# Six pairs of the attention's output columns by seven products, with sums and forms on POOL, and two merge columns moved

## The chip, the cores and the metric

The kernel runs on one core of a Trainium2 chip. The metric is device time in microseconds for one execution. The engines are named as in the profile: PE is TensorE (matmuls), DVE is VectorE, ACT is ScalarE, POOL is GpSimd, SP is SyncE, which here issues the DMA transfers. SBUF is the on-chip memory that the engines work in, PSUM the banks in which PE adds up products.

## The reference

One layer of a hybrid encoder in fp32, for 512 prompt tokens and 8 x 16 sample tokens; the kernel takes them as T = 640 columns. Cut to what matters:

```
z = x @ w_in                                   # x: 640 x 2048
y_a = (fox_attention(q, k, v, f) * silu(gate_a)) @ w_out_fox     # 1024 -> 2048
y_b = (gated_delta(conv(qkv), g, beta) * silu(gate_b)) @ w_out_gdn   # 1024 -> 2048
h = (sigmoid(m_a) * y_a + sigmoid(m_b) * y_b) @ w_out            # 2048 -> 2048
x1 = layer_norm(alpha * x + h)
out = x1 + sigmoid(x1 @ w_pl_gate) * rms_norm(p @ w_pl_proj)
```

Both branches have 8 heads of 128. The delta branch solves a triangular system per chunk and head and carries a state from chunk to chunk. m_a and m_b, the merge gates, are columns of the first product.

## The kernel before, in words

**Products.** Activations lie with features on the 128 partitions and the 640 tokens along the free dimension, in two halves of 320. Every fp32 operand is split in a rounded part (a cast on ACT) and the rest (a subtraction on DVE): `split`, L333 and L334, makes xh and xl of a tile of activations; `w_piece`, L305 and L306, makes wh and wl of a weight piece of 128x512. A product of two tiles is three matmuls: wh by xh, wh by xl, wl by xh.

**Weights** come as halves of 512 KB (`wr`, three buffers, L252, issued by SP), in an order fixed by `plan`. `w_ahead`, called ahead of each k-tile, starts a load when a buffer is free and cuts pieces up to five (`PIECES`) ahead of their use.

**Columns.** `column` (L359 and L360) makes one block of 128 output features: 16 k-tiles by 3 matmuls by 2 token halves, 96 matmuls. `pair` (L433) makes two blocks by Strassen's and Winograd's seven products in place of eight: the operands are four sub-blocks of activations and sums of them (X11, X21, X22 and T1 to T4, called forms), and four sums of weight halves (S1, S2, b, S3). The results are added up on DVE (L442). In the kernel before, the front, w_out and the gate use `pair`; weight sums of the front are made on DVE, those of the later pairs ahead of time on POOL (`weight_sums`, L272), by way of DRAM.

**Stages.** The front; the attention with its 8 heads; the delta branch (`phase_gdn`), for each of 8 heads four columns and one merge column (`mcol`, `FILL` = 1); two more merge columns; the attention's output columns (w_out_fox, K = 1024), 16 blocks, each 48 matmuls in a group of 8 k-tiles, copied by ACT (`kept`, tile fx, L1522) and stored in DRAM (fd); then the delta output columns, w_out, norm and gate.

**Order.** Beside PE's columns run generators: conv_silu, the head's preparation (`gdn`), its blocks (`gdn_blocks`), its chunks (`gdn_chunks`), the output norm. `tick`, once per k-tile or so, steps them when a clock kept while the program is built (`saw` adds a cost for each instruction, `watch` compares) says that what they issue will be ready. On the chip there are only in-order queues and semaphores. `gdn_blocks` is the one the change and the prediction touch: it writes the lower blocks to DRAM and reads them back as `lanes`, runs a scan of 31 steps on DVE (two operations each, L933 and L935, sx and sx2, ever shorter), writes the result (`xd<-sx`, L941), reads it back as u0 (L944) and loads the state (L948). Behind it in `gdn_chunks` each chunk makes right sides rp (L1110) and the state S (L1124) on DVE, for which PE's small matmuls wait.

The inputs of the output columns, the heads' results og, are kept in DRAM (`ogd`); 16 tiles are reloaded (`ogr<-ogd`, L1492) and split.

Of the kernel before, what the change touches and what calls it, by code (L numbers as in the profile page):

```python
# [52 lines left out]
class Kernel:  # L53
# [9 lines left out]
    PAIR0, PAIRS = 10, 4 + FRONT // 2  # L63
    FILL = 1
    GATES = 6
    FREE = 0.5
    LATE = 3
# [9 lines left out]
    def saw(self, ins):  # L77
# [14 lines left out]
        if e == 3:  # L92
# [101 lines left out]
    def plan(self):  # L194
# [4 lines left out]
        self.ops, self.halves, c = [], [], 0  # L199
        self.wsums, self.later = {}, [*range(n - 32, n - 16, 2), *range(n - 16 + self.GATES, n, 2)]  # L200
        while c < n:
            if c in self.later:
# [31 lines left out]
            c += len(cs)  # L234
        self.raw, self.wq, self.used = {}, {}, 0
        self.rest = 0
        self.nh = self.no = self.np = 0

    def w_new(self, tag):
        pool = self.wp if tag == "wr" else self.zp  # L240
        return pool.tile([P, 1024], F32, tag=tag, name=tag, bufs=3)

    def w_tile(self):
        c, hf, tag, uses = self.halves[self.nh]
        self.nh += 1
        self.raw[c, hf] = [self.w_new(tag), uses, tag]
        return c, hf

# [31 lines left out]
    def w_free(self, tag):  # L280
        return sum(v[1] > 0 for v in self.raw.values() if v[2] == tag) < 3

# [26 lines left out]
    def w_ahead(self):  # L309

        if self.nh < len(self.halves) and self.now >= self.rest and self.w_free(self.halves[self.nh][2]):
            self.w_load()
        if self.no == len(self.ops):
            return
        o = self.ops[self.no]
        if o[0] == "s":
            if o[2] in self.raw and o[3] in self.raw and (o[1] in self.raw or self.w_free("sr")):
                self.no += 1
                self.w_sum(*o[1:])
        elif self.np - self.used < self.PIECES and o[1] in self.raw:  # L320
            self.w_piece()
# [5 lines left out]

    def split(self, src):

# [3 lines left out]
        nc.scalar.copy(out=hi, in_=src)  # L333
        nc.vector.tensor_tensor(out=lo, in0=src, in1=hi.bitcast(F32), op=ALU.subtract)  # L334
        return hi, lo
# [75 lines left out]

    def pair(self, xf, fin, each=None, uv=None):


        nc = self.nc
        c = self.col
        self.col += 2
        u, v = uv or (self.zt([P, HALF], "u"), self.zt([P, HALF], "v"))
        banks = {}

        def run(i, form, bank, more=False):
            if not more:
                banks[bank] = self.gps(xf[form][0][0].shape[-1])
            ps = banks[bank]
            for k in range(8):
                if each:
                    each(i, k)
                self.w_ahead()
                wh, wl = self.wq[(c, i), k // 4]
                w = slice((k % 4) * P, (k % 4) * P + P)  # L430
                xh, xl = xf[form][k]
                for n, (a, b) in enumerate(((wh, xh), (wh, xl), (wl, xh))):
                    nc.tensor.matmul(ps, a[:, w], b, start=(k == 0 and n == 0 and not more), stop=(k == 7 and n == 2),  # L433
                                     skip_group_check=True)
# [9 lines left out]
        w = body(u)  # L444
        add(w, w, run(1, "T2", "b"))
        fin(0, 0, run(2, "X21", "a", True))
        add(v, w, body(run(3, "T3", "d")))
# [469 lines left out]
    def gdn_blocks(self, h, kq, lt, qk, qg, kt, vr, cs):  # L917
# [30 lines left out]
        nc.sync.dma_start(out=st, in_=self.i["st"][h])  # L948
        yield 8
        self.chunks["gens"].append(self.gdn_chunks(h, kq, lt, qk, qg, kt, vr, cs, u0, st))  # L950

# [16 lines left out]
    def gdn_out(self, h, ob, cs):  # L968
# [30 lines left out]
        if h < 7:  # L999
            nc.sync.dma_start(out=self.ogd[8 + h], in_=og)  # L1000
        else:
            self.op[15] = self.split(og)
        self.gdone = h
# [436 lines left out]
    def phase_gdn(self, conv, work):  # L1440
# [6 lines left out]
        self.sums["gens"].append(self.weight_sums([ws[:, x:x + 171] for x in range(0, 684, 171)], slice(8, None),  # L1447
                                                  (10, 8, 5)))
        self.uu = self.zt([P, 5, P], "uu")
# [9 lines left out]
        self.gdone = -1  # L1459
        self.scaled, self.chdone = False, -1  # L1460
        self.ends["gens"].append(self.scale_e(re))
        self.untapped = 0
        for h in range(H):
# [24 lines left out]
        due = deque()  # L1488

        def load(k, tag):  # L1490
            raw[k] = self.zt([P, T], tag, 1, "ogr")
            nc.sync.dma_start(out=raw[k], in_=self.ogd[k])  # L1492
            if k < 8:
                due.append((self.now + 8, k))

        def each1(s):
# [3 lines left out]
            if s in (8, 10, 12):  # L1500
                load((s - 8) // 2, tags[(s - 8) // 2])
        tags = "strip", "cy", "sg"

        def take():
            k = due.popleft()[1]
            nop[k] = self.split(raw[k])
            if k + 3 < 8:
                load(k + 3, tags[k % 3])

        def after(s):  # L1510
            if due and due[0][0] <= self.now and due[0][1] <= s:
                take()
        self.mcol("cth", each=each1)
        self.mcol("cth", after=after)
# [4 lines left out]
        def kept(ps):  # L1519
# [4 lines left out]
            self.nf += 1  # L1524
        for n in range(8):
            def each(s):
                while n == 0 and due and (due[0][0] <= self.now or due[0][1] <= s):
                    take()
                k = 8 + n
                if s == 1 and n < 7:  # L1530
                    self.until(lambda: self.gdone >= n)
                    load(k, ("sg", "cth")[n % 2])
                if s == 13 and n < 7:
                    nop[k] = self.split(raw[k])
# [587 lines left out]
def _layout(a):  # L2122
# [13 lines left out]
          for g in range(2)]  # L2136
    nf, r = Kernel.FRONT, Kernel.FILL
    bl += [bq[0], bk[0], *bv[0], *bv[1]]
# [9 lines left out]
    for h in range(H):  # L2148
        bl += [gq[h], gv[h], gk[h], gg[h]]
        if h < 7:  # L2150
            bl += m[nf + 3 + r * h:nf + 3 + r * (h + 1)]
    bl += m[nf + 3 + 7 * r:]
    for n in ("w_out_fox", "w_out_gdn"):
        wo = _wblock(a[n][0])
        bl += [np.concatenate([wo[2 * i], wo[2 * i + 1]], 1) for i in range(8)]
    for b in _wblock(a["w_out"][0]):
# [71 lines left out]
```

## Time and profile before

| what | us |
|---|---|
| runs shown, median (lowest to highest) | 2203.46 (2202.28 to 2206.6) |
| profiled execution, its own time | 2205.76 |
| span of the profile | 2202.9 |
| PE busy in the span | 2186.2 |
| DVE / ACT / POOL busy | 1488.9 / 901.3 / 317.0 |

| stretch of the span, us | DVE busy | ACT busy | POOL busy |
|---|---|---|---|
| 950 to 1540, delta heads and merge columns | 426.89 | 254.78 | 97.17 |
| 1540 to 1667, attention's output columns | 64.96 | 47.48 | 12.83 |
| 1667 to 2203, the rest | 436.25 | 230.75 | 64.54 |

The profile is of one execution; the granted TensorE clock was 0.998 over it. A row of a group says line, engine, operation, out<-in, shapes and count, then busy time and mean ns of one, then the engine's idle time just before and what ended it. In a timeline the first number is the start, the second the length, and x2 means that two neighbours are shown as one.

### The profile page before, as it was taken

To read this page: it belongs to the slowest core of one execution; us is meant where nothing else is said; L and a number is where in the kernel's file an instruction comes from. 1 tells how busy PE (TensorE), PEld (TensorE's weight loads), DVE (VectorE), ACT (ScalarE), POOL (GpSimd) and SP (SyncE) were. 2 spreads that over 40 slices of the span, in tenths; PEclk is the share of its full clock that TensorE was granted. 3 is DMA by queue.
4 is the path that set the end of the run, shared out by engine and by line. 5 is a ranking of instruction groups with operands and counts; after the bars stand their busy time and mean duration, and the time that the engine had idled before them with its cause. 6 is when DMAs were issued, how large, how long until landed. Compare 5 with 4: busy or idle time off the path is not lost. (4 is left out here: it accounts for less than half of the span.)

```text
span 2202.9 us, 41346 instructions
## 1 busy us (share of the span) xinstructions
PE 2186.2 (99%) x15586; PEld 2110.7 (96%) x15586; DVE 1488.9 (68%) x3055; ACT 901.3 (41%) x2007; POOL 317.0 (14%) x530
## 2 busy tenths in 40 slices
PE   9999999999999999999999999999999999999998
PEld 7889999999999999999999999999999999999998
DVE  5377777664454446666776866767645787789997
ACT  4244444443333335334434534435332243354544
POOL 0003222220101000111111211111100000021222
PEclk9999999999999999999999999999999999999999
DMA  6336555657877657834434434446646656673465
GB/s 234 125 123 196 190 187 190 198 187 247 274 232 264 226 173 242 282 107 139 139 114 137 132 107 142 126 123 193 196 151 216 220 160 210 193 274 130 147 227 170
DMA packets 205799, 403.25 MB, mean 183 GB/s; under 512 B 32392, under 2 KB 104152, under 8 KB 205600
## 3 DMA queue, kind: packets, MB, share of 16 engines
q1 hardware_dynamic: 205600, 400.62, 56.4%
q8 instruction: 122, 2.00, 0.4%
q14 instruction: 77, 0.63, 0.1%
HBM read 310.97 MB, written 89.56 MB: 182 GB/s over the span
## 5 line engine op out<-in xcount | busy, mean ns | idle before, releaser
L306 DVE TENSOR_TENSOR wl<-wr,wh 128x512 fp32r<-128x512 f32 x634 | 457.3, 731 | 367.8 <-ACT wh L305 362.2
L305 ACT CAST wh<-wr 128x512 fp32r<-128x512 f32 x634 | 389.1, 620 | 379.5 <-PE g L360 156.1
L359 PE MATMUL g<-xh,wh 128*128 128x320 f32 (+1 forms) x1312 | 427.2, 326 | 0.8 <-ACT xh L333 0.4
L359 PE MATMUL g<-xl,wh 128*128 128x320 f32 (+1 forms) x1312 | 405.9, 309 | 0.5 <-DVE xl L334 0.5
L360 PE MATMUL g<-xh,wh 128*128 128x320 f32 x1312 | 405.8, 309 | 0.0
L360 PE MATMUL g<-xl,wh 128*128 128x320 f32 x1312 | 405.5, 309 | 0.0
L359 PE MATMUL g<-xh,wl 128*128 128x320 f32 (+1 forms) x1312 | 405.4, 309 | 0.0
L360 PE MATMUL g<-xh,wl 128*128 128x320 f32 x1312 | 405.2, 309 | 0.0
L433 PE MATMUL g<-xh,wh 128*128 128x320 f32 (+1 forms) x864 | 267.6, 310 | 2.6 <-ACT u L443 1.1
L433 PE MATMUL g<-xl,wh 128*128 128x320 f32 (+1 forms) x864 | 267.7, 310 | 0.6 <-DVE xl L334 0.6
L433 PE MATMUL g<-xh,wl 128*128 128x320 f32 (+1 forms) x864 | 267.5, 310 | 0.0
L359 PEld LDWEIGHTS g<-xh,wh 128*128 128x128 f32 x1312 | 247.3, 189 | 13.8 <-issue 9.5
L360 PEld LDWEIGHTS g<-xh,wh 128*128 128x128 f32 x1312 | 247.5, 189 | 0.9
L359 PEld LDWEIGHTS g<-xl,wh 128*128 128x128 f32 x1312 | 247.2, 188 | 1.1 <-DVE xl L334 1.1
L360 PEld LDWEIGHTS g<-xl,wh 128*128 128x128 f32 x1312 | 247.0, 188 | 0.0
L359 PEld LDWEIGHTS g<-xh,wl 128*128 128x128 f32 x1312 | 246.6, 188 | 0.2 <-DVE wl L306 0.2
L360 PEld LDWEIGHTS g<-xh,wl 128*128 128x128 f32 x1312 | 246.7, 188 | 0.0
L272 POOL TENSOR_TENSOR ws<-ws 128x171 f32<-128x171 f32 (+2 forms) x176 | 128.0, 727 | 809.3 <-DMA ws<-in_w 800.8
L433 PE MATMUL g<-t,wh 128*128 128x320 f32 (+1 forms) x848 | 187.7, 310 | 0.4 <-ACT t L2045 0.4
L433 PEld LDWEIGHTS g<-xh,wh 128*128 128x128 f32 x864 | 162.6, 188 | 3.5 <-ACT u L443 1.4
L433 PEld LDWEIGHTS g<-xl,wh 128*128 128x128 f32 x864 | 162.4, 188 | 1.2 <-DVE xl L334 1.1
L433 PEld LDWEIGHTS g<-xh,wl 128*128 128x128 f32 x864 | 162.7, 188 | 0.0
(425 smaller groups left out, 3469.8 us busy)
## 6 DMA issues: line engine op xcount, KB each, us to landing
wr<-in_w SPq DMA_DIRECT2D x263, 512.0 KB, 3.8
kc<-in_kc SPq DMA_DIRECT2D x32, 512.0 KB, 7.4
vc<-in_vc SPq DMA_DIRECT2D x32, 512.0 KB, 5.8
ws<-in_w SPq DMA_DIRECT2D x80, 128.0 KB, 2.5
md<-m SPq DMA_DIRECT2D x32, 320.0 KB, 2.3
t<-md SPq DMA_DIRECT2D x32, 320.0 KB, 4.6
ws<-in_w SPq DMA_DIRECT2D x100, 85.5 KB, 3.4
t<-rr SPq DMA_DIRECT2D x24, 320.0 KB, 5.5
```

The source lines that it names most:

```text
L272: nc.gpsimd.tensor_tensor(out=o, in0=x, in1=y, op=op)
L305: nc.scalar.copy(out=hi, in_=src)
L306: nc.vector.tensor_tensor(out=lo, in0=src, in1=hi.bitcast(F32), op=ALU.subtract)
L359: nc.tensor.matmul(ps[0], whl[w], xhl[o][:, a], start=(first and x == 0), stop=(last and x == 2))
L360: nc.tensor.matmul(ps[1], whl[w], xhl[o][:, b], start=(first and x == 0), stop=(last and x == 2))
L433: nc.tensor.matmul(ps, a[:, w], b, start=(k == 0 and n == 0 and not more), stop=(k == 7 and n == 2), skip_group_check=True)
```

## The change

1. `FILL` becomes a table for each head: heads 5 and 6 lose their merge column, which then run behind head 7's columns, ahead of the two that were there.
2. The first two of the eight pairs of attention's output blocks stay plain (`PLAIN`). The other six run as half pairs: `pair(half=True)`, seven products of 4 k-tiles, 84 matmuls for two blocks. The order of products is X11, T2, T1, T3, X21, X22, T4.
3. The four weight sums of each half pair are made on POOL, 128x512 each (`m_sum`), just ahead of use, into tiles that earlier work has left (`ws`, `sg` and the raw halves, later loads of which go to `kq0` and `lanes`).
4. The forms are made by a new generator, `forms`: it reloads eight og tiles, makes four sums of 128x320 for each two k-tiles on POOL (`form_sums`), and splits them on ACT, DVE and POOL (`form_splits`).
5. Of the delta branch's og tiles, reloaded during the half pairs, those of even index are split in the last half pair with the rest on POOL; the last head's og is split after the loop. The clock's cost of a POOL operation and the waits of `weight_sums` change, and with them where generators are stepped.

```diff
-    FILL = 1
+    FILL = 1, 1, 1, 1, 1, 0, 0, 4
+    PLAIN = 2
...
-        a, b = ((0.17, 0.0011), (0.21, 0.00085), (0.25, 0.0020))[e]
+        a, b = ((0.17, 0.0011), (0.21, 0.00085), (0.13, 0.0032))[e]
...
+            if n - 48 + self.PLAIN <= c < n - 40:
+                j = c - (n - 48 + self.PLAIN)
+                self.halves += [(c, 0, "wr", 5), (c, 1, "wr" if j < 2 else ("kq0", "lanes")[j % 2], 3)]
+                for key, p, i in (((c, 0), 0, 0), ((c, "S2"), 0, 1), ((c, "S1"), 0, 4), ((c, "b"), 0, 3),
+                                  ((c, 0), 1, 2), ((c, "S3"), 0, 6), ((c, 1), 1, 5)):
+                    self.ops.append(("p", key, p, ((c, i), 0)))
+                self.sumq += [(c, x) for x in ("S1", "S2", "b", "S3")]
...
+    def m_sum(self):
+        c, name = self.sumq[0]
...
+        lo, hi = slice(0, 512), slice(512, 1024)
+        a = self.w_use((c, 0)) if name != "S1" else None
+        b = self.w_use((c, 1)) if name in ("S1", "b") else None
...
+        self.raw[c, name] = [out, uses, "m"]
+        self.nc.gpsimd.tensor_tensor(out=out, in0=x, in1=y, op=op)
+        self.made[c, name] = self.busy[2] + 0.3
...
+        if half:
+            add(v, w, run(4, "T1", "c"))
+            add(v, v, run(3, "T3", "d"))
+            fin(1, 1, v)
+            fin(0, 0, run(2, "X21", "a", True))
+            fin(0, 1, run(6, "X22", "c", True), u)
+            fin(1, 0, run(5, "T4", "d", True), u)
+            return
...
-            for _ in range(self.FILL if h < 7 else 0):
+            for _ in range(self.FILL[h] if h < 7 else self.FILL[7] - 2):
                 self.mcol("sg")
...
+        def form_sums(k):
+            a, b = fr[2 * k], fr[2 * k + 1]
+            for o, x, y, op in ((b[:, xb], b[:, xb], a[:, xb], ALU.subtract), (a[:, xb], a[:, xb], a[:, xa], ALU.subtract),
+                                (a[:, xa], b[:, xb], a[:, xa], ALU.add), (b[:, xa], b[:, xa], a[:, xa], ALU.subtract)):
+                nc.gpsimd.tensor_tensor(out=o, in0=x, in1=y, op=op)
+        def form_splits(k):
+            a, b = fr.pop(2 * k), fr.pop(2 * k + 1)
+            th, tl = self.split(b, nc.gpsimd)
...
+            for t, sl in ((t1, xb), (t2, xa)):
+                nc.scalar.copy(out=t[:, xa], in_=a[:, sl])
+                nc.vector.tensor_tensor(out=t[:, xb], in0=a[:, sl], in1=t[:, xa].bitcast(F32), op=ALU.subtract)
...
-        for n in range(8):
+        for n in range(self.PLAIN):
...
+        self.until(lambda: len(xf["X11"]) == 4)
...
+        for n in range(self.PLAIN, 8):
...
+            self.pair(xf, kept2, each, uv=(uv, fx[1][:, xb]), half=True)
+            self.nf += 2
```

The change moves instructions on three engines in one place, the last delta head's scan. In what follows, lines of the kernel before and of the change differ in number: L933 and L935 are now L992 and L994, L941, L944 and L948 now L1000, L1003 and L1007, L252 is L267, L306 is L351, L272 is L287.

POOL, around head 7's scan, before (uu and kpad are copies for a head's chunks, vm is a masked product, ws a weight sum):

```order
L962 COPY uu<-u_17721 32x5x32 x4
L272 TENSOR_TENSOR ws<-ws 128x171 x2
L1026 TENSOR_TENSOR vm<-vnd,cb 128x256
L272 TENSOR_TENSOR ws<-ws 128x171 x10
L957 COPY kpad<-kq_9603 128x4x16 x2
```

The same place now:

```order
L1022 COPY uu<-u_17819 32x5x32 x4
L1592 TENSOR_TENSOR ogr<-ogr 128x320 x4
L1086 TENSOR_TENSOR vm<-vnd,cb 128x256
L1592 TENSOR_TENSOR ogr<-ogr 128x320 x4
L381 TENSOR_TENSOR xl<-ogr,xh 128x640 x2
L339 TENSOR_TENSOR s_18308<-wr 128x512
L339 TENSOR_TENSOR s_18320<-s_18308,wr 128x512
L339 TENSOR_TENSOR wr<-wr 128x512
L1592 TENSOR_TENSOR ogr<-ogr 128x320 x4
L339 TENSOR_TENSOR s_18320<-wr,s_18320 128x512
L1592 TENSOR_TENSOR ogr<-ogr 128x320 x4
L381 TENSOR_TENSOR xl<-ogr,xh 128x640 x2
```

The form sums (L1592), their splits (L381) and the first half pair's weight sums (L339) stand where twelve sums of 128x171 stood; those now stand ahead.

DVE, the part of head 7's scan in which the chunks of head 6 are made, before:

```order
L1124 SCALAR_TENSOR_TENSOR S<-S,gl,s 128x128
L306 TENSOR_TENSOR wl<-wr,wh 128x512
L933 TENSOR_TENSOR sx_18263<-sx,lanes 80x8x27
L935 TENSOR_TENSOR sx<-sx,sx_18263 80x8x27
L933 TENSOR_TENSOR sx_18263<-sx,lanes 80x8x26
L935 TENSOR_TENSOR sx<-sx,sx_18263 80x8x26
L1110 SCALAR_TENSOR_TENSOR rp<-s,negc,vr 128x128
```

The same now:

```order
L1182 COPY S<-s 128x128
L1107 SCALAR_TENSOR_TENSOR st<-st,glb,s 128x128 x4
L1602 TENSOR_TENSOR t_18232<-ogr,t_18232 128x320
L1602 TENSOR_TENSOR t_18233<-ogr,t_18233 128x320
L992 TENSOR_TENSOR sx_18146<-sx,lanes 80x8x25
L994 TENSOR_TENSOR sx<-sx,sx_18146 80x8x25
L992 TENSOR_TENSOR sx_18146<-sx,lanes 80x8x24
L994 TENSOR_TENSOR sx<-sx,sx_18146 80x8x24
L351 TENSOR_TENSOR wl<-wr,wh 128x512
L1170 SCALAR_TENSOR_TENSOR rp<-s,negc,vr 128x128
```

The splits of t1 and t2 (L1602) and the state updates st now stand between the scan's steps and ahead of rp.

SP, from the scan's write to the weight loads, before:

```order
L941 DMA xd<-sx 80x256
L252 DMA wr<-in_w 128x1024
L1523 DMA fd_18012<-fx 128x640
L944 DMA u_18679<-xd 128x5x32
L948 DMA st<-in_st 128x1024
```

The same now:

```order
L1000 DMA xd<-sx 80x256
L1193 DMA out_stp<-S 128x128
L1032 DMA og<-sgd_174 128x640
L1003 DMA u_18682<-xd 128x5x32
L1007 DMA st<-in_st 128x1024
L267 DMA wr<-in_w 128x1024 x2
```

A weight half that stood between write and read-back is now behind both and the state's load.

More of the change, by code (lines that the diff above doesn't have):

```diff
@@ L424, in run @@
             ps = banks[bank]
-            for k in range(8):
+            last = 3 if half else 7
+            for k in range(last + 1):
                 if each:
@@ L432, in run @@
                 for n, (a, b) in enumerate(((wh, xh), (wh, xl), (wl, xh))):
-                    nc.tensor.matmul(ps, a[:, w], b, start=(k == 0 and n == 0 and not more), stop=(k == 7 and n == 2),
+                    nc.tensor.matmul(ps, a[:, w], b, start=(k == 0 and n == 0 and not more), stop=(k == last and n == 2),
                                      skip_group_check=True)
@@ L1001, in gdn_out @@
         else:
-            self.op[15] = self.split(og)
+            self.last = og
         self.gdone = h
@@ new lines, in forms @@
+        def forms():
+            while self.sums["gens"]:
+                yield 1
+            load2(0, "ws")
+            load2(1, "og")
+            while self.done[0] < 7:
+                yield 1
+            load2(2, "dt")
+            load2(3, "v")
+            yield 4
+            form_sums(0)
+            yield 2
+            form_sums(1)
+            yield 2
+            while self.op is not nop or due:
+                yield 1
+            load2(4, "cth")
+            form_splits(0)
+            load2(5, "og")
+            self.formed = True
+            yield 1
+            form_splits(1)
+            load2(6, "dt")
+            load2(7, "v")
+            yield 5
+            form_sums(2)
+            yield 1
+            form_sums(3)
+            form_splits(2)
+            yield 1
+            form_splits(3)
+            yield 1
@@ L1524, in kept @@
             self.nf += 1
-        for n in range(8):
+        for n in range(self.PLAIN):
             def each(s):
-                while n == 0 and due and (due[0][0] <= self.now or due[0][1] <= s):
+                while n == 0 and due and (due[0][0] <= self.now or order[due[0][1]] <= s):
                     take()
[L1529 to L1534, printed above, removed]
-            self.column(groups=((0, 8), (8, 16)), base=0, each=each, done=kept)
+            self.column(groups=((0, 8), (8, 16)), base=0, each=each, done=kept)
@@ new lines, in store, with each @@
+        def store():
+            while late:
+                i, t = late.popleft()
+                nc.sync.dma_start(out=self.fd[i], in_=t)
+        again = dict(zip(range(8, 15), ("dt", "v", "kt", "vr", "lt", "qk", "gr")))
+        for n in range(self.PLAIN, 8):
+            def each(i, k):
+                if (i, k) == (1, 0):
+                    store()
+                if n in (5, 6) and k == 0 and i in (2, 3, 4, 5):
+                    x = 4 * n - 14 + i
+                    if x < 15:
+                        self.until(lambda: self.gdone >= x - 8)
+                        load(x, again[x])
+                if n == 7 and k == 2 and i in (1, 4, 3, 2):
+                    x = {1: 8, 4: 10, 3: 12, 2: 14}[i]
+                    nop[x] = self.split(raw[x], nc.gpsimd)
+                if n == 7 and i == 5:
+                    x = 9 + 2 * k
+                    if x < 15:
+                        nop[x] = self.split(raw[x])
+            fx[1] = self.zt([P, T], "cy", 1, "fx")
+            self.pair(xf, kept2, each, uv=(uv, fx[1][:, xb]), half=True)
+            self.nf += 2
@@ L1536, in phase_gdn @@
+        store()
+        self.until(lambda: self.gdone == 7)
+        nop[15] = self.split(self.last)
         self.until(lambda: self.gdone == 7 and not self.sums["gens"])
```

113 lines of the change are left out of this document (88 added, 25 removed).

## The prediction

> **What bounds the kernel now.** I read the page's busy shares first, then the chain of waits, then the windows over the stage that is changed, and last the timelines of the two engines that share work there.
>
> ```profile
> span 2202.9 us, 41346 instructions
> PE 2186.2 (99%) x15586; PEld 2110.7 (96%) x15586; DVE 1488.9 (68%) x3055; ACT 901.3 (41%) x2007; POOL 317.0 (14%) x530
> ```
>
> TensorE (PE) is busy for 2186.2 of 2202.9 us. Fewer matmuls are therefore worth their whole time, and every new wait of PE is lost whole. The price of one matmul stands in the chain of waits (start, us, what), where PE runs products of the pair form without a break:
>
> ```profile
> 1809.22 170.03 PE g L433 x1158
> ```
>
> That is 170.03 / 1158 = 0.147 us for a matmul of 320 columns. The stage that changes is the attention's output columns and the end of the last delta head, from about 1500 to 1670 us. Its windows show (range, length, then busy us and count of PE, PEld, DVE, ACT, POOL, then clock, DMA share, GB/s):
>
> ```profile
> 1500.00:1550.00 50.00, 49.83 (x398) 46.68 (x397) 33.15 (x100) 28.26 (x77) 9.19 (x17) 1.00 0.69 210
> 1550.00:1600.00 50.00, 50.00 (x397) 49.47 (x395) 36.80 (x108) 19.70 (x53) 7.45 (x16) 1.00 0.64 197
> 1600.00:1650.00 50.00, 50.00 (x371) 47.99 (x364) 18.85 (x50) 19.74 (x54) 2.98 (x5) 1.00 0.47 153
> ```
>
> PE is full, at a granted clock of 1.00. VectorE (DVE) has 17 and 13 us of 50 free up to the end of the last head's scan, and 31 after it; GpSimd (POOL) does almost nothing.
>
> **The matmuls.** Each of the six half pairs runs seven products of 4 k-tiles by 3 matmuls, 84, where two plain columns ran 96. The small matmuls stay in number, and so do the merge columns, which only change place. So 6 x 12 = 72 matmuls go: 72 x 0.147 = **-10.6 us**. Heads 5 and 6 lose 96 matmuls (14.1 us) of PE work each, under which DVE works. By the row of 1500 to 1550 DVE is busy for two thirds of the time there, so I cost the loss of this cover at nothing; if it is short, PE waits in those heads for states or pieces, up to 2 us.
>
> **Steady work of the half pairs.** DVE cuts seven pieces a pair instead of four, ScalarE (ACT) too:
>
> ```profile
> L306 DVE TENSOR_TENSOR wl<-wr,wh 128x512 fp32r<-128x512 f32 x74 | 51.9, 701 | 61.8 <-ACT wh L305 60.9 <-DMA wr<-in_w 0.7
> L764 DVE SCALAR_TENSOR_TENSOR sg<-sc,sg 128x320 f32<-128x320 f32 x2 | 1.0, 491 | 0.1
> L272 POOL TENSOR_TENSOR ws<-ws 128x171 f32<-128x171 f32 x100 | 67.1, 671 | 224.7 <-DMA ws<-in_w 219.2
> L2042 POOL TENSOR_TENSOR t<-t 128x640 f32<-128x640 f32 x20 | 36.2, 1815 | 68.5 <-DMA t<-rr 37.1 <-DVE wl L306 15.4 <-DVE t L2010 15.1
> ```
>
> A pair lasts 84 x 0.147 = 12.3 us on PE. DVE needs 7 x 0.70 for pieces and at most 7 x 0.49 for additions of 320 columns, 8.3 us; ACT is given three casts more, and had 30 of 50 us free in the row of 1600. POOL makes four sums of 128x512. No such POOL row exists: between 0.671 us (171 columns) and 1.815 us (640) a straight line gives 1.50, so 6.0 us a pair. The last pair has four lo splits of 640 columns on POOL instead, 7.3 us. All of it fits under 12.3 us of PE, so I cost it at nothing; if the first splits of the next column come late there, PE loses 1 to 2 us. The eight reloads of 320 KB lie ahead of their readers by ticks of the plan and cost nothing either, unless SP is held up (below).
>
> **The stretch in which the forms are made** is another matter. Between the start of head 7's scan and the last form split (t2 of the fourth k pair, which the first half pair's second product, T2, needs), the order has 174 matmuls of 320 columns and 25 small ones on PE; on DVE 56 scan operations, 7 pieces, 8 splits of 320 and 15 operations of 128x128; on POOL 8 form sums of 320, 4 weight sums of 512 and 4 splits of 640. The rows for these:
>
> ```profile
> 1062.34 0.38 PE L1106 MATMUL s<-S,kq 128*128 128x128 f32 x2
> L933 DVE TENSOR_TENSOR sx<-eye,lanes 80x248 f32<-80x248 f32 x1 | 0.4, 405 | 0.0
> L933 DVE TENSOR_TENSOR sx<-sx,lanes 80x32 f32<-80x32 f32 x1 | 0.2, 188 | 0.0
> L1110 DVE SCALAR_TENSOR_TENSOR rp<-s,negc,vr 128x128 f32<-128x128 f32 x3 | 1.0, 344 | 1.7 <-PE s L1106 1.7
> ```
>
> PE: 174 x 0.147 + 25 x 0.19 = 30.3 us. DVE: the scan shortens from 0.405 to 0.188 us an operation, 56 x 0.297 = 16.6, and 7 x 0.70 + 8 x 0.49 + 15 x 0.344 = 14.0, together 30.6 us. So DVE has no spare time here, where it had a quarter in the rows above. And the two engines hold each other up. Both timelines (start, us, engine, line, xcount) are of the kernel before:
>
> ```profile
> 1060.88 2.02 POOL L272 TENSOR_TENSOR ws<-ws 128x171 f32<-128x171 f32 x3
> ...
> 1061.27 0.60 DVE L933 TENSOR_TENSOR sx<-sx,lanes 80x152 f32<-80x152 f32 x1
> ...
> 1062.54 0.53 DVE L933 TENSOR_TENSOR sx<-sx,lanes 80x144 f32<-80x144 f32 x1
> ...
> 1063.10 0.30 DVE L935 TENSOR_TENSOR sx<-sx,sx 80x144 f32<-80x144 f32 x1
> ```
>
> ```profile
> 2085.79 3.79 POOL L2042 TENSOR_TENSOR t<-t 128x640 f32<-128x640 f32 x2 [0.18 <-DMA t<-rr]
> 2086.08 4.05 DVE L306 TENSOR_TENSOR wl<-wr,wh 128x512 fp32r<-128x512 f32 x2
> ...
> 2089.93 3.60 POOL L2042 TENSOR_TENSOR t<-t 128x640 f32<-128x640 f32 x2 [0.35 <-DMA t<-rr]
> 2090.45 3.63 DVE L306 TENSOR_TENSOR wl<-wr,wh 128x512 fp32r<-128x512 f32 x2
> 2090.67 0.39 PE L433 MATMUL g<-xh,wh 128*128 128x320 f32 x1 [0.94 <-ACT t L2045]
> ```
>
> A scan operation takes 0.60 beside a POOL sum of 171 columns and 0.30 without: 0.3 us lost for each. A piece takes 2.03 beside a POOL operation of 640 columns instead of 0.70: 1.33 lost. On the line between them 320 columns cost 0.63 and 512 cost 1.05. The 16 POOL operations then cost 8 x 0.63 + 4 x 1.05 + 4 x 1.33 = 14.6 us, if DVE always stands at an operation with two inputs in SBUF. The scan, the pieces and the splits are that, 25.4 of 30.6 us, the 128x128 ones read PSUM; so 14.6 x 0.83 = 12.1. DVE ends 12.4 us behind PE's 30.3. How much of that PE bears: in the second timeline DVE lost (4.05 + 3.63) - 4 x 0.70 = 4.9 us, and PE's own gap, 0.94, was for another engine. I let PE bear 4.9 and take **+7.5 us**, with 0 and 12.4 as its bounds. What comes late is the states and right sides of head 6's chunks (S, rp), for which PE stands, and behind them in DVE's queue its pieces and t2. A single rule of the Trainium skill speaks to this more strictly; it stands with the rivals.
>
> **The weight load behind the scan's end.** In the new order the load of the second half pair's half stands on SP behind the scan's write, the og load, the read-back and the state load; before, it stood ahead of the read-back. SP's waits, from the chain:
>
> ```profile
> 1514.41 3.44 DMA xd<-sx
> ...
> 1517.87 0.37 SPq L944
> ...
> 1518.28 1.16 SPq L948
> ...
> 1519.54 5.50 DMA wr<-in_w
> ```
>
> That landing is a long one by the page's list of transfers (last column: median us to landing):
>
> ```profile
> wr<-in_w SPq DMA_DIRECT2D x263, 512.0 KB, 3.8
> ```
>
> From the scan's end to the landed half: 3.44 + 0.37 + 1.16 + 3.8 to 5.5, 8.8 to 10.5 us. Then S1 and S2 on POOL (3.0) and the cast on ACT (0.6, estimated from DVE's 0.70) make 12.4 to 14.1. The scan ends six scan operations and a piece after t2 is split, 6 x 0.19 + 0.70 = 1.8 us. From T2 of the first pair, where it needs that t2, to T2 of the second PE has 74 matmuls, 10.9 us. So PE waits 1.8 + 12.4 - 10.9 = 3.3 to 5.0 us if it stood at t2, and as much less as it came later than t2. I take **+3.2**, bounds 0 and 5. Queued behind that load on SP are only loads and fx stores; later pairs load before the sums that need them and gain slack.
>
> Sum: -10.6 + 7.5 + 3.2 = +0.1 us. The profiled run of before took 2205.76 us, 2.86 around its span and 2.3 over the median; against the median the forecast is 2203.46 + 0.1 = 2203.5, **about 2203.5 us: no change**.
>
> **Rivals.** (A) *POOL's work falls where DVE waits anyway.* For it: DVE stood idle 60.9 us for ACT's casts before its 74 pieces from 1400 to 1700 us, and a late DVE is allowed what PE holds in cut pieces, which the second timeline shows to be at least 4.9 us. Then the stretch costs 0.6 and the load 3.2: -10.6 + 3.8 = -6.8, 2196.7 us. Against it: no idle time is left in that stretch by the sum above.
>
> (B) *The whole POOL operation blocks DVE,* in that one stretch. A DVE operation then loses all of a POOL operation's time; from the rows 0.671 and 1.815 a line gives 1.03 for 320 columns and 1.50 for 512, so 8 x 1.03 + 4 x 1.50 + 4 x 1.815 = 21.5, times 0.83 is 17.8 us. DVE ends 18.1 late, PE bears 4.9 and stops for 13.2; with the load's 3.2 the sum is -10.6 + 16.4 = +5.8: 2209.3 us, slower. It decides once the stretch and the load cost more than 10.6. For it, the 4.05 us of two pieces beside 3.79 of two POOL operations; against it, that POOL's own times in these rows already hold its waits for DVE. The Trainium skill, "SBUF — State Buffer", section "SBUF: two separate sides", says of the port pair that DVE and GpSimd share that it is an exclusive lock, held for the whole instruction by whichever starts first, and counts DVE operations with two SBUF inputs among its takers. By that rule (B) is the case, and the sum would be 2209; the 0.60 against 0.30 us in the first timeline agrees in kind, with a smaller loss.
>
> (C) *Everything hides:* both waits fit into slack, the 72 matmuls are all: 2192.9 us. Against it stands the SP order alone.
>
> **How the numbers follow.** The likeliest is the sum, 0.43, own range 2199 to 2208 (the load at 0 or 5, the stretch 3 us either way). (A) has 0.26, (B) 0.23, (C) and the like 0.08. A measurement of this kernel tells about 0.2%, 4.4 us, from no change. Faster: (A), (C), and a little of the first, 0.33; slower: (B) and a little of the first, 0.26; the same 0.41. The range leaves (C) out below and ends above (B): 2195 to 2210.
>
> **What would show it.** Right: 72 fewer matmuls at 0.147 us; PE gaps that name S, rp or t2 as releaser while POOL runs form sums, 4 to 10 us in all; one gap of 1 to 5 us at the second half pair's T2 ended by wh or wl; scan operations beside POOL at 0.6 to 1.3 us instead of 0.3. (A) shows PE without gaps in the stretch, (B) scan operations that take 1 us and more and gaps over 12 us. Wrong altogether: gaps in heads 5 and 6 or in the columns after the last pair, or POOL sums of 512 columns over 2.5 us, so that a pair is held by POOL.

## The result and the profile after

| kernel | median us (lowest to highest) | ratio to the kernel before, 95% interval |
|---|---|---|
| before | 2202.28 (2200.30 to 2206.60) | 1 |
| changed | 2214.14 (2212.09 to 2217.66) | 1.0055 [1.0039, 1.0071] |

The change makes the kernel slower, by 12 us (9 to 16 by the interval). The forecast was 2203.5 with a range of 2195 to 2210, so it missed. The profiled execution of the changed kernel took 2217.66 us against 2205.76, and its span is 12.9 us longer. First the page of the changed kernel:

```profile
span 2215.8 us, 41390 instructions
PE 2185.5 (99%) x15514; PEld 2108.4 (95%) x15514; DVE 1538.3 (69%) x3107; ACT 912.3 (41%) x2025; POOL 377.2 (17%) x578
```

The matmuls fell from 15586 to 15514, by 72 as counted, and yet PE's busy time hardly moved (2186.2 to 2185.5): what PE saved in number it gave back in speed, as the clock below shows. The windows over the changed stage, columns as in the prediction:

```profile
1500.00:1550.00 50.00, 48.78 (x388) 46.09 (x386) 35.81 (x96) 26.04 (x60) 13.74 (x15) 1.00 0.64 205
1550.00:1600.00 50.00, 43.64 (x278) 41.78 (x278) 42.57 (x108) 17.24 (x49) 17.76 (x16) 0.90 0.38 122
1600.00:1650.00 50.00, 47.55 (x359) 44.55 (x360) 32.78 (x59) 20.77 (x51) 25.60 (x25) 0.93 0.44 150
1650.00:1700.00 50.00, 50.00 (x343) 49.97 (x342) 41.51 (x74) 21.26 (x40) 13.50 (x8) 1.00 0.64 227
```

From 1550 to 1650 PE does 637 matmuls where it did 768 before, stands still for 8.8 us, and runs at a mean clock of 0.90 and 0.93 instead of 1.00. The waits of PE from 1470 to 1670 us, with what ended them (us in total, times, longest), without two of 0.2; the kernel before has none in that range:

```profile
PE s L1166 <- DVE S L1184: 5.3, 2, 3.6
PE s L1166 <- DVE S L1182: 3.5, 1, 3.5
PE g L484 <- ACT wh L350: 2.6, 1, 2.6
```

They are four places: head 5's S at 1478 us (1.8 of the 5.3), S twice behind the start of head 7's scan, at 1548 and 1572, and a cast wh at 1599, for the second half pair's T2. Around the first S of head 7's stretch, DVE and then POOL:

```profile
1546.06 0.39 DVE L992 TENSOR_TENSOR sx<-sx,lanes 80x232 f32<-80x232 f32 x1
1546.49 1.65 DVE L994 TENSOR_TENSOR sx<-sx,sx 80x232 f32<-80x232 f32 x1
...
1549.02 1.64 DVE L992 TENSOR_TENSOR sx<-sx,lanes 80x216 f32<-80x216 f32 x1
...
1551.81 0.28 DVE L1182 COPY S<-s 128x128 f32<-128x128 f32 x1
...
1554.23 1.32 DVE L994 TENSOR_TENSOR sx<-sx,sx 80x200 f32<-80x200 f32 x1
...
1572.31 0.91 DVE L992 TENSOR_TENSOR sx<-sx,lanes 80x120 f32<-80x120 f32 x1
```

```profile
1546.32 1.57 POOL L381 TENSOR_TENSOR xl<-ogr,xh 128x640 fp32r<-128x640 f32 x1 [2.02 <-ACT xh L380]
...
1554.00 1.33 POOL L339 TENSOR_TENSOR s<-wr 128x512 f32<-128x512 f32 x1 [3.58 <-DVE t L1602]
...
1570.24 3.77 POOL L1592 TENSOR_TENSOR ogr<-ogr 128x320 f32<-128x320 f32 x4
```

A scan operation that starts during a POOL operation ends about a quarter of a microsecond after it: 1546.32 + 1.57 = 1547.89, and DVE's ends at 1548.14. It takes 1.65 beside 640 columns, 1.32 beside 512 and 0.91 beside 320, where the neighbours without POOL take 0.39, 0.35 and 0.29. S of the next chunk is queued behind these on DVE.

The chain at the fourth place, from the scan's end to the piece that T2 needs (start, us, what):

```profile
1589.47 1.66 DMA xd<-sx
...
1591.18 0.37 SPq L1003
...
1591.60 0.51 SPq L1007
...
1592.21 6.58 DMA wr<-in_w
...
1598.95 1.23 POOL s L339
...
1601.56 0.63 ACT wh L350
...
1602.21 1.10 DVE wl L351
```

And what stood in no term of the prediction, windows of 5 us that begin 2.6 to 6.5 us after a gap of PE began (the third number from the right is the granted clock):

```profile
1555.00:1560.00 5.00, 5.00 (x21) 5.00 (x20) 4.93 (x9) 0.62 (x1) 4.84 (x5) 0.50 0.00 0
...
1575.00:1580.00 5.00, 3.71 (x18) 3.71 (x19) 4.34 (x12) 0.62 (x1) 0.54 (x1) 0.75 0.01 3
...
1605.00:1610.00 5.00, 5.00 (x58) 4.34 (x56) 2.25 (x5) 0.00 (x0) 3.56 (x6) 0.68 0.00 0
```

PE is full from 1555 to 1560 and does 21 matmuls, at a clock of 0.50. Matmuls of 320 columns start every 0.267 us there instead of 0.147. Beyond the normal spacing the three stretches cost 1.9, 1.4 and 1.0 us.

The account of PE's time in this one execution, from the starts of its matmuls: -10.6 for 72 matmuls; +1.9 for head 5's S; +7.4 for the two S behind head 7's scan start (gaps of 3.77 and 3.90); +3.2 for T2 (2.80 and 0.69); +4.3 for the half clock after these; +2.7 in the norm near 2100 us, where a gap of 2.54 stands against 1.25 before and has a half clock of 1.4 behind it. That is +8.9; the other 4.0 of the 12.9 are small waits and small matmuls at the low clock, which I did not take apart. The account says where PE's time went, not what each part would give back if it were gone. The part at 2100 us does not go with the half pairs: in the profiled executions of the kernels below that gap is 0 to 2.58 us, 1.18 and 1.26 in two that have six half pairs (change_no_move, sums_act) and 2.56 in moved, which has none.

### The profile page after: what moved, and what is told of

Its sections match the earlier page's. It is cut to its first block, busy times and chain, and to the rows that moved or that the text cites. A ratio compares the mean times of both kernels' runs of the same rounds, so it can differ in the third digit from the quotient of the medians.

```text
span 2215.8 us, 41390 instructions
## 1 busy us (share of the span) xinstructions
PE 2185.5 (99%) x15514; PEld 2108.4 (95%) x15514; DVE 1538.3 (69%) x3107; ACT 912.3 (41%) x2025; POOL 377.2 (17%) x578
## 4 chain that ended last, share of the span: by engine, by line
PE 91%; DVE 4%; DMA 3%; ACT 1%; issue 1%; SPq 0%; POOL 0%; DVEq 0%; ACTq 0%; POOLq 0%
PE g L484 31%; PE g L406 24%; PE g L407 23%; PE g L450 4%; DMA wr<-in_w 1%; PE s L450 1%; PE s L786 1%; PE s L962 1%; DVE wl L351 1%; PE s L742 1%; DVE sx L992 1%; PE s L701 1%; DVE sx L994 1%; DMA lanes<-ld 0%; DMA kc<-in_kc 0%
## 5 line engine op out<-in xcount | busy, mean ns | idle before, releaser
L351 DVE TENSOR_TENSOR wl<-wr,wh 128x512 fp32r<-128x512 f32 x626 | 458.1, 741 | 325.6 <-ACT wh L350 319.5
L406 PE MATMUL g<-xh,wh 128*128 128x320 f32 (+1 forms) x1216 | 397.1, 327 | 0.7 <-ACT wh L350 0.7
L406 PE MATMUL g<-xl,wh 128*128 128x320 f32 (+1 forms) x1216 | 377.2, 310 | 0.5 <-DVE xl L381 0.5
L407 PE MATMUL g<-xh,wh 128*128 128x320 f32 x1216 | 377.0, 310 | 0.0
L406 PE MATMUL g<-xh,wl 128*128 128x320 f32 (+1 forms) x1216 | 376.9, 310 | 0.0
L407 PE MATMUL g<-xl,wh 128*128 128x320 f32 x1216 | 376.9, 310 | 0.0
L407 PE MATMUL g<-xh,wl 128*128 128x320 f32 x1216 | 376.6, 310 | 0.0
L484 PE MATMUL g<-xh,wh 128*128 128x320 f32 x984 | 307.4, 312 | 3.9 <-DVE t L493 2.2
L484 PE MATMUL g<-xl,wh 128*128 128x320 f32 x984 | 305.7, 311 | 0.6 <-DVE xl L381 0.6
L484 PE MATMUL g<-xh,wl 128*128 128x320 f32 x984 | 305.7, 311 | 0.0
L287 POOL TENSOR_TENSOR ws<-ws 128x171 f32<-128x171 f32 (+2 forms) x176 | 123.8, 704 | 786.6 <-DMA ws<-in_w 776.5
L406 PEld LDWEIGHTS g<-xh,wh 128*128 128x128 f32 x1216 | 230.3, 189 | 12.8 <-issue 8.2
L407 PEld LDWEIGHTS g<-xh,wh 128*128 128x128 f32 x1216 | 230.5, 190 | 0.9
L406 PEld LDWEIGHTS g<-xl,wh 128*128 128x128 f32 x1216 | 229.9, 189 | 1.0 <-DVE xl L381 1.0
L407 PEld LDWEIGHTS g<-xl,wh 128*128 128x128 f32 x1216 | 229.9, 189 | 0.0
L406 PEld LDWEIGHTS g<-xh,wl 128*128 128x128 f32 x1216 | 229.5, 189 | 0.1
L407 PEld LDWEIGHTS g<-xh,wl 128*128 128x128 f32 x1216 | 229.5, 189 | 0.0
L484 PE MATMUL g<-t,wh 128*128 128x320 f32 (+1 forms) x944 | 211.7, 313 | 3.1 <-ACT wh L350 2.6
L484 PEld LDWEIGHTS g<-xh,wh 128*128 128x128 f32 x984 | 186.1, 189 | 5.3 <-ACT wh L350 2.5
L484 PEld LDWEIGHTS g<-xl,wh 128*128 128x128 f32 x984 | 185.8, 189 | 1.2 <-DVE xl L381 1.0
L484 PEld LDWEIGHTS g<-xh,wl 128*128 128x128 f32 x984 | 186.0, 189 | 0.0
```

The lines of the kernel that those rows point to most:

```text
L287: nc.gpsimd.tensor_tensor(out=o, in0=x, in1=y, op=op)
L406: nc.tensor.matmul(ps[0], whl[w], xhl[o][:, a], start=(first and x == 0), stop=(last and x == 2))
L407: nc.tensor.matmul(ps[1], whl[w], xhl[o][:, b], start=(first and x == 0), stop=(last and x == 2))
```

## The experiments

The theory (L) was the prediction's: POOL's two-input operations hold DVE for nearly their whole length, S comes late, PE stands. Its rivals: (D) DVE lacks time there whoever makes the forms, (M) moving the merge columns made the gaps. All ratios are to the kernel before, run on the same chip. Lines of the experiments can be off by up to 10 from those of the change.

**1. The forms nearly taken off POOL** (forms16). The form sums work on 16 of 320 columns, so the forms are not the reference's, and POOL's eight lo splits of 640 are replaced by copies on ACT; the planned costs, and so the order, stay.

```diff
-                nc.gpsimd.tensor_tensor(out=o, in0=x, in1=y, op=op)
+                nc.gpsimd.tensor_tensor(out=o[:, 0:16], in0=x[:, 0:16], in1=y[:, 0:16], op=op)
...
-        (eng or nc.vector).tensor_tensor(out=lo, in0=src, in1=hi.bitcast(F32), op=ALU.subtract)
+        if eng:
+            nc.scalar.copy(out=lo, in_=src)
```

> The change with its form sums cut to 16 of 320 columns and with the eight lo splits of POOL replaced by plain copies on ACT, at the same planned cost: PE, DVE and SP hold the same instructions in the same order. Theory L (POOL's operations hold up DVE's two-input operations): scan operations beside POOL fall back to 0.3 to 0.4 us outside the weight sums, the two gaps of 3.8 and 3.9 us for S go or fall under 1 us, and with them the half clock that follows them (1.9 and 1.4 us): about 10 us less, 2204 us; the gap of 2.8 us at the second half pair's T2 stays. Rival D (DVE is late from its own added splits and the late read-back of the lanes): both gaps stay, 2212 to 2215 us.

Measured 2204.50 us, ratio 0.9998 [0.9989, 1.0006]: 12.6 us less than the change by the ratios. Windows of the same 130 us in the kernel before, the change and this one:

```profile
1540.00:1670.00 130.00, 130.00 (x977) 126.03 (x976) 65.65 (x177) 48.42 (x127) 12.83 (x24) 1.00 0.52 165
```

```profile
1540.00:1670.00 130.00, 119.97 (x845) 114.03 (x845) 101.06 (x215) 53.74 (x134) 58.54 (x51) 0.93 0.45 151
```

```profile
1540.00:1670.00 130.00, 124.81 (x908) 119.63 (x908) 97.60 (x225) 64.51 (x152) 40.46 (x41) 0.97 0.46 158
```

PE does 63 matmuls more in the window than in the change. DVE had the same operations to do, and head 7's scan, from its first operation to its last, took 38.3 us instead of 46.8, so (D) falls for this stretch. The gaps did not vanish: 2.46 us for rp at 1552, and two that make 2.5 for T2 at 1590, stay.

**2. The weight sums taken off POOL** (sums_act). The four sums of each half pair become copies of one operand on ACT, so the products are not the reference's.

```diff
-        self.nc.gpsimd.tensor_tensor(out=out, in0=x, in1=y, op=op)
+        self.nc.scalar.copy(out=out, in_=y)
```

> The change with the 24 weight sums replaced by copies of 512 columns on ACT (0.62 us by its row, POOL 1.27), same planned cost and same order on PE, DVE and SP. Theory L: the four sums in the stretch held DVE for 4 x 1.0 us, so the gaps for S shrink by 3 to 4 us together, perhaps one falls under the length that halves the clock; the gap at T2 shrinks by 2 x 0.65 = 1.3 us: 2207 to 2210 us. Rival D: only the 1.3 us at T2, 2213 us.

Measured 2217.09 us, ratio 1.0057 [1.0043, 1.0071], as the change; the expectation missed. The S gap at 1546 stayed (3.95 us), the second S gap went and one of 1.04 for rp stands near it, but T2 still waits 2.98, and new gaps of 1.76 and 1.96 us came. The copies wait for weight loads in ACT's queue, and the casts behind them wait too. The edit mixes two things and settles nothing.

**3. The clock kept up** (warm). Dummy matmuls stand ahead of the three late products (22, 22 and 16 of them), in the PSUM bank that the product then overwrites, so that PE works through its waits.

```diff
+                if h == 6 and t in (1, 3):
+                    self.warm(pd[:, 0:HALF], 22)
...
+            if half and i == 1 and c == self.i["w"].shape[0] // 2 - 47 + self.PLAIN:
+                self.warm(ps, 16)
```

> The change with dummy matmuls of 320 columns queued on PE ahead of the three late matmuls (22, 22 and 16 of them, into the bank that the next product overwrites), nothing else. Theory C (the half clock follows from the gap itself, 1.9, 1.4 and 1.0 us, and slower small matmuls): granted clock stays 1.00 from 1550 to 1610, the last matmul of each group still waits as long, 4 to 6 us less, 2208 to 2210 us. Rival (the clock falls for another reason, such as load on the other engines): no change, 2214 us.

Measured 2214.62 us, ratio 1.0040 [1.0027, 1.0053]. Against the change's 1.0055 that is 3.3 us less, not the 4 to 6 expected, and the intervals overlap. The same window:

```profile
1540.00:1670.00 130.00, 125.93 (x923) 120.56 (x922) 105.54 (x217) 55.71 (x137) 62.09 (x53) 0.99 0.44 149
```

The clock is 0.99 instead of 0.93, and of 4.3 us lost to the half clock 0.6 are left. A gap of 2.52 us for rp is still there. The two traces also tell where a faster PE helps. The S that ends the gap of 1572 is made at 1575.9 us in the change and at 1575.6 here; T2 of the second half pair begins at 1602.2 and 1601.6, T2 of the third at 1623.8 and 1620.7. Ahead of the second T2 most of the time won is waited away again, since DVE's scan (46.8 and 46.5 us long) and the load behind it set the pace there; behind it 2.5 us stay won. So the trace shows the loss, and its size in time, some 3 us, is only made likely.

**4. The move alone** (moved). The kernel before, with the merge columns of heads 5 and 6 behind head 7's.

```diff
-    FILL = 1
+    FILL = 1, 1, 1, 1, 1, 0, 0, 4
```

> The kernel before with only the two merge columns moved from heads 5 and 6 to behind head 7, everything else as before. Theory L: costs little, the one gap of 2 us for S at head 6's scan, 2202 to 2205 us. Rival M (heads 5 and 6 without their column are what makes DVE late in the last scan): gaps over 2 us also behind head 7, 2207 us and more.

Measured 2208.88 us, ratio 1.0016 [1.0007, 1.0025]: 3.5 us slower (1.5 to 5.5), a time that I had given to (M). But behind head 7 there is no gap, so (M) falls. At head 5 there is one of 2.18 us and a half clock of 1.2 behind it. The chain there, and the wait it makes (two views):

```profile
1470.00 0.32 SPq L1472
...
1470.51 5.04 DMA lanes<-ld
```

```profile
PE s L1106 <- DVE S L1124: 1.9, 1, 1.9
```

The scan's lanes take 5.04 us to come back from DRAM. SP issued that load at 1470.51, behind a store of the head's gate (L1472), for which it stood 5.4 us: 7.5 us after the last of the writes to DRAM, where the kernel before has 1.5 (1456.75 to 1458.24). DVE stands idle for 3.2 us until the lanes are there, and head 5's S then stands behind eight scan operations. So what the move took away is the order of SP's queue as much as the work on PE that covered the load.

**5. Four half pairs, with the forms on POOL and on DVE** (plain4, forms_dve4). The first leaves four of the eight pairs plain. The second also makes the form sums and the forms' lo splits on DVE; both leave nothing of the reference out.

```diff
-    PLAIN = 2
+    PLAIN = 4
```

```diff
-                nc.gpsimd.tensor_tensor(out=o, in0=x, in1=y, op=op)
+                nc.vector.tensor_tensor(out=o, in0=x, in1=y, op=op)
...
-            th, tl = self.split(b, nc.gpsimd)
+            th, tl = self.split(b)
```

> The change with four plain pairs and four half pairs in place of two and six; forms on POOL as before, made at the same place. Theory L (the forms on POOL hold DVE, once): the gaps for S of 3 to 4 us with their half clock are there although no half pair runs yet; the gap at a half pair's T2 goes, two pairs' gain of 3.5 us goes with it: 2211 to 2216 us against 2203 of before. Rival P (each half pair costs more than it saves, by its seven pieces and four sums): two thirds of the loss stay, and the gaps stand in the pairs, not in the columns ahead, about 2207 us.

> Form sums and the lo splits of the forms on DVE instead of POOL, planned with DVE's cost, and four half pairs. Theory L: on DVE a sum of 320 takes 0.48 us and a split of 640 0.74, less than the 0.63 and 1.25 us that DVE loses beside POOL's, so DVE needs 6.8 us for them in the stretch instead of 10; no gap over 1 us behind head 7. 48 matmuls less are -7.1, the gap at 1477 us with its half clock +3.1, others +1: ratio to before about 0.9986. Rival D (DVE is full there anyway): S comes late as before, gaps of 3 to 4 us, ratio 1.003 and more.

Measured: plain4 2212.89 us, 1.0041 [1.0029, 1.0054]; forms_dve4 2199.74 us, **0.9977 [0.9967, 0.9987]**, faster than both kernels. Two pairs fewer gave nothing that the intervals tell apart from the change; the engine of the forms made 14 us. PE's longest waits from 1470 to 1670, plain4 first:

```profile
PE s L1166 <- DVE S L1182: 3.6, 1, 3.6
PE s L1166 <- DVE S L1184: 3.3, 2, 1.8
```

```profile
PE s L1166 <- DVE S L1184: 1.2, 1, 1.2
PE g L406 <- DVE xl L381: 0.8, 1, 0.8
```

The S waits behind head 7 are gone although DVE now does more (the 1.2 is head 5's). A form sum takes DVE 0.49 us, and cost it 0.62 when POOL made it. That one edit also shifts the planned order: during the scan PE starts 280 matmuls of 320 columns instead of plain4's 193. So not all of the 14 us is proven to be the lock.

**6. Five half pairs, and a filled gap at head 5** (forms_dve3, forms_dve4_warm). The first is forms_dve4 with PLAIN = 3; the second is forms_dve4 with ten dummy matmuls ahead of head 5's late S.

```diff
-    PLAIN = 4
+    PLAIN = 3
```

```diff
+                if h == 5 and t == 3:
+                    self.warm(pd[:, 0:HALF], 10)
```

> The same with five half pairs. Theory L: 60 matmuls less, -8.8, with 3.1 for the gap at 1477 us and 2 to 3 for waits at the first half pair, which comes 14 us earlier: ratio 0.998 to 0.999. Rival D: 1.004.

> As four half pairs with forms on DVE, and ten dummy matmuls ahead of the third product with the state in head 5, where the gap at 1477 us stands. Theory C (a gap of about 2 us is followed by 3 us of half clock): the clock stays at 1.00 there, 1.0 to 1.4 us less than without, ratio 0.998. Rival: the clock falls all the same, no difference.

Measured: forms_dve3 2203.42 us, 0.9992 [0.9983, 1.0001]; forms_dve4_warm 2201.20 us, 0.9981 [0.9972, 0.9989]. The fifth half pair gains nothing and seems to cost 3 us, but the intervals just overlap, and forms_dve3's profile has the gap at 2085 us with its half clock, which forms_dve4's has not. The dummies fill the gap at 1477 and gain nothing that can be measured; in forms_dve4's profile no half clock followed that gap.

**7. The change itself with its forms on DVE** (forms_dve2): the second diff of 5 on the change, six half pairs.

> The changed kernel with one thing other: the 16 form sums and the forms' four 640-column lo splits are made by VectorE instead of GpSimd; six half pairs, weight sums on GpSimd, merge columns as in the change. Theory L (GpSimd's two-input operations hold VectorE for nearly their whole length): VectorE does this work itself in 16 x 0.48 + 4 x 0.74 = 10.6 us less than nothing gained, where standing still for it cost 16 x 0.63 + 4 x 1.25 = 15 us, so a ratio to the kernel before 0.003 to 0.005 under that of the change: 1.000 to 1.003, with at most one gap of more than 2 us for S behind head 7's scan start. Rival D (VectorE is short of time there whoever does the work): no better than the change, 1.0045 to 1.007, gaps for S as long as there.

Measured 2218.62 us, ratio 1.0064 [1.0052, 1.0077]: no better than the change. The time is the one of (D) and not of (L). The waits of PE from 1470 to 1670 tell more than the time:

```profile
PE g L484 <- ACT wh L350: 7.0, 4, 4.4
PE g L484 <- DVE wl L351: 7.0, 5, 5.9
PE s L1166 <- DVE S L1184: 1.1, 1, 1.1
```

The S waits behind head 7 are gone, where (D) had them as long as in the change; two other waits took their place. One stands in the last half pair, where POOL makes four lo splits of the delta branch's tiles. DVE and POOL there:

```profile
1659.51 1.54 DVE L1039 TENSOR_TENSOR ms<-ms,cs 128x5 f32<-128x5 f32 x1
1661.08 1.50 DVE L1040 TENSOR_TENSOR ms<-ms,cs 128x5 f32<-128x5 f32 x1
1662.61 1.47 DVE L1041 TENSOR_SCALAR ms<-ms 128x5 f32<-128x5 f32 x1
...
1665.61 0.17 DVE L186 TENSOR_SCALAR rfy<-rft 128x5 int32<-128x5 int32 x1
```

```profile
1658.98 6.57 POOL L381 TENSOR_TENSOR xl<-ogr,xh 128x640 fp32r<-128x640 f32 x4
```

Operations of five columns take 1.5 us until POOL is done (L1041 takes 0.17 at 1592 us, where POOL does nothing), and the piece behind them comes 5.9 us late for PE. The other wait, 4.67 us at 1599 us, is for the weight load of the third half pair's T2, which stands on SP behind the scan's write (9). The scan ends late here, for a reason that the edit brought with it. Where its last step stands on DVE:

```profile
1589.62 0.17 DVE L994 TENSOR_TENSOR sx<-sx,sx 80x16 f32<-80x16 f32 x1
...
1595.26 0.16 DVE L992 TENSOR_TENSOR sx<-sx,lanes 80x8 f32<-80x8 f32 x1
```

Between them stand pieces, sums of a half pair and the 128x5 operations of a head's norm, 5.5 us in all, where the change has 0.5. In the order that is planned with the forms on DVE the scan's steps stand further apart: the scan lasts 57.5 us instead of 46.8, and DVE hardly pauses in it. So (D) is wrong about S, but with six half pairs it isn't refuted for this wait: DVE's queue is full there with the forms on either engine.

**8. The merge columns put back** (change_no_move, forms_dve4_no_move): the change, and forms_dve4, with heads 5 and 6 keeping theirs.

```diff
-    FILL = 1, 1, 1, 1, 1, 0, 0, 4
+    FILL = 1, 1, 1, 1, 1, 1, 1, 2
```

> The changed kernel with its two merge columns put back to heads 5 and 6; half pairs, forms and sums as in the change. If the move costs what it cost alone in the kernel before (+3.5 us), and nothing else depends on it: 2210 to 2211, ratio 1.0035 to 1.0045, no gap at head 5's S near 1478, the gaps behind head 7 as before. Rival: the moved columns cover the work on the forms and weight sums behind head 7, so that without them the gaps there grow by more than the 3.5 us won: ratio 1.0055 or over.

> Four plain columns and four half pairs, form sums and forms' lo splits on VectorE, and the two merge columns back at heads 5 and 6. If the move costs 3.5 us by itself and VectorE still has room behind head 7: 2196 to 2197, ratio 0.996 to 0.997, no gap at head 5's S. Rival: VectorE lacks the time that the two moved columns gave it behind head 7: ratio 0.998 to 1.001, with gaps for S, rp or wl between 1540 and 1670 us.

Measured: change_no_move 2220.97 us, 1.0080 [1.0066, 1.0094]; forms_dve4_no_move 2206.61 us, 1.0010 [1.0001, 1.0018]. Both times the rival held (the intervals of the first and of the change just overlap, those of the second and of forms_dve4 don't). The gap at head 5 is gone, but in the first PE now waits for the forms themselves, from 1470 to 1670:

```profile
PE g L484 <- DVE t L1602: 11.4, 2, 6.3
PE s L1174 <- DVE rp L1170: 5.2, 2, 2.6
```

So the move costs 3.5 us by itself and inside the change more likely wins, some 5 us, as work on PE under which DVE catches up. In forms_dve4_no_move the one large gap, 6.48 us at 1655, stands beside POOL's four lo splits again.

**9. Those four lo splits on DVE too** (dve2_nosplit, dve4_no_move_nosplit, dve4_nosplit): forms_dve2, forms_dve4_no_move and forms_dve4, each with this.

```diff
-                    nop[x] = self.split(raw[x], nc.gpsimd)
+                    nop[x] = self.split(raw[x])
```

> forms_dve2 with the last half pair's four lo splits of 640 columns on VectorE too. If GpSimd's splits held VectorE's short operations there (6.25 us gap of PE and 2.04 us of half clock behind it), it is some 6 to 8 us faster than forms_dve2's 1.0064: ratio 1.0028 to 1.0037, no gap over 2 us near 1662. Rival (VectorE is short of time there whoever does the work): ratio 1.005 or over, a gap for wl of more than 3 us in the same place.

> forms_dve4_no_move with the last half pair's four lo splits on VectorE. If GpSimd's splits made the 6.48 us gap near 1655 and the 1.32 us of half clock behind it: 6 to 8 us under that kernel's 1.0010, ratio 0.9975 to 0.9985. Rival (VectorE is short of time): ratio 0.9995 or over.

> forms_dve4 (ratio 0.9977, only 1.09 us of gap near 1661) with the last half pair's four lo splits on VectorE. There is little to win: ratio 0.9970 to 0.9980. It would be worse, 0.999 or over, if VectorE lacked the 4 x 0.74 = 3.0 us there.

| kernel | us | ratio, 95% interval | gap near the last half pair: before this edit, with it |
|---|---|---|---|
| dve2_nosplit | 2213.75 | 1.0038 [1.0026, 1.0051] | 6.25, 1.68 us |
| dve4_no_move_nosplit | 2202.54 | 0.9993 [0.9984, 1.0001] | 6.48, 2.93 us |
| dve4_nosplit | 2200.29 | 0.9980 [0.9971, 0.9988] | 1.09, 0.98 us |

The first wins 5.7 us as a ratio, a little under the 6 to 8 expected, the second 3.7 with half of its gap left, between the two expectations, the control nothing. POOL's splits made most of the first gap and over half of the second; what is left there isn't taken apart. In dve2_nosplit what is left is the weight load of a half pair's T2, a gap of 4.76 us. SP's waits from 1570 to 1610, and the landing in the chain:

```profile
SPq L1000 <- DVE sx L994: 12.1, 1, 12.1
```

```profile
1599.83 4.18 DMA wz<-in_w
```

SP stood 12.1 us at the write of the scan's result (L1000), with the load of wz right behind it; it was issued as soon as SP was free. Whether its buffer had come free earlier, the trace doesn't tell. The scan's last step is late here as in forms_dve2, 5.8 us behind the step before it, so SP's order and DVE's make this gap together.

## Why the prediction failed

**What bounds the kernel, and the matmuls (-10.6).** Right: 72 fewer, every new wait of PE lost whole.

**Heads 5 and 6, costed at nothing, "up to 2 us" if short.** Wrong: 3.5 us alone (4), 1.9 plus a share of small waits in the change. I judged the cover by DVE's busy share over 50 us. What lost its cover was one load of 5 us, issued late behind a store on SP, and the order of DVE's queue behind it, which no share shows. That the moved columns would win time behind head 7 (8) was in no term either.

**Steady work of the half pairs, nothing.** Right as far as the rows show it, from the third half pair on: the row of 1650 to 1700 has PE full at a clock of 1.00. POOL's sums of 512 columns took 1.29 us, less than the 1.50 taken.

**The stretch of the forms, +7.5.** Right in place and releaser: S, twice. The size, 7.4 us, is in part luck. DVE's own share was well priced: from the scan's first operation to the last split of t2 it took 45.2 us, 2.0 of them idle, where the sum has 42.7. But the 4.9 us that PE was to bear came from another place of the kernel, and no run measures them here. The lock cost 0.62, 0.97 and 1.26 us an operation for 320, 512 and 640 columns (0.91 - 0.29, 1.32 - 0.35, 1.65 - 0.39), priced at 0.63, 1.05 and 1.33. That it is this lock is shown by experiments 1, 5 and 7, where the S waits behind head 7 shrink or go with POOL's forms alone. A form sum and a split of 640 cost DVE more this way than doing the work itself (0.49 and 0.82 us in forms_dve4).

**The weight load behind the scan's end, +3.2.** Right in size, with luck: 2.80 and 0.69 us of gaps, 3.2 beyond the normal spacing. From the scan's end to the cast piece it took 12.7 us, within the 12.4 to 14.1, but the write took 1.66 instead of 3.44 and the load 6.58 instead of 3.8 to 5.5, two errors that cancel. The named cause, SP's order, isn't proven in the change, since a piece of DVE that may have freed the load's buffer ended at 1592.04, just when SP came to it. In dve2_nosplit SP's wait of 12.1 us ahead of such a load is in the trace.

**The missing step: the clock.** No term had what PE loses behind a gap. PE's matmuls of 320 columns took 4.3 us more for it in the stretch; by experiment 3 some 3 us, small matmuls included, are time, most of it behind the second half pair's T2. The kernel before already showed it: at 535 us PE stands twice, 1.83 and 1.32 us with 0.7 us of small matmuls between, and from 540.4 to 543.6 it does twelve matmuls at 0.267 us. I read the mean clock of 0.998 and not that place (the kernel before):

```profile
535.00:540.00 5.00, 1.85 (x13) 1.38 (x12) 3.29 (x11) 2.46 (x9) 0.16 (x1) 1.00 0.98 365
540.00:543.00 3.00, 3.00 (x14) 3.00 (x13) 1.39 (x3) 1.28 (x4) 2.77 (x5) 0.56 0.19 74
```

The Trainium skill, "TensorE: Matmul & The Clock Gate", Part 1, gives about 3.4 us of idle time as what drops the clock to half; here single gaps of 2.54 us (the change, at 2099 us) and 2.18 us (moved, at 1477 us) were followed by it, and one of 2.06 us (the change, at 1478 us) was not.

**Rivals.** (A) and (C) fell. (B), 2209.3, was on the right side and had the stronger form of the lock: a DVE operation ends 0.25 us behind the POOL operation it met. The Trainium skill's rule of an exclusive lock ("SBUF — State Buffer", section "SBUF: two separate sides") agrees with that. But (B)'s 13.2 us of standing was 7.4; its nearness to the time is luck, since the clock and heads 5 and 6, which make up the rest, were not in it.

The sum that failed was -10.6 + 7.5 + 3.2 = +0.1. With head 5 (+1.9) and the clock (+4.3 of PE's time) it is +6.3; the tail's +2.7 belongs to one execution, and 4.0 are not taken apart. So about half of the 12 us is named: the clock behind the gaps and the lost cover of heads 5 and 6, both costed at nothing. Which of the small waits the change makes in every execution stays open.

## What to carry to other kernels

Moving two-input work from a busy DVE to an idle POOL is no gift: price each such operation at what DVE loses beside it, and compare that with DVE doing it itself. A PE gap can cost more than its length when the clock halves behind it, so add that to any wait of 2 us and more that a change introduces, unless PE would wait again soon after for the same other engine. Before filler work is moved, look at which transfer it covers, what stands ahead of that in the issuing queue and behind it in the waiting engine's, not at the busy share.

## What the hardware showed that I had not expected

The half clock does not follow from a gap's length alone. The same gap at the same place, 2.53 to 2.58 us in the norm between 2084 and 2102 us, occurs in the profiles of twelve of these sixteen kernels; in seven PE then ran some 3.2 us at half clock (some 1.4 us lost), in five not. For example in moved and in dve4_nosplit, windows of 5 us:

```profile
2090.00:2095.00 5.00, 2.75 (x19) 2.51 (x18) 5.00 (x4) 2.44 (x4) 4.92 (x3) 1.00 0.53 183
2095.00:2100.00 5.00, 5.00 (x35) 5.00 (x35) 4.90 (x10) 1.34 (x3) 0.30 (x1) 1.00 0.59 203
```

```profile
2085.00:2090.00 5.00, 2.76 (x18) 2.53 (x17) 5.00 (x5) 1.54 (x2) 3.93 (x3) 0.93 0.52 186
2090.00:2095.00 5.00, 5.00 (x27) 5.00 (x27) 4.40 (x10) 1.24 (x2) 0.00 (x0) 0.73 0.57 189
```

Where it came, it came late: PE ran at full clock again for 0.5 to 1.5 us before the clock fell. And DVE's operations of 128x5, also those with one tensor operand (L1041), were held by POOL like large ones, 1.47 us instead of 0.17 (forms_dve2, at 1662 and at 1592 us).
